# Seven products of halves in the first 16 feature tiles of a down projection

## The chip, the core and the metric

The kernel runs on one core of a Trainium2 chip. The metric is the device time of one execution in microseconds (us), as the median of several runs. TensorE multiplies into PSUM, VectorE and ScalarE read PSUM and work on SBUF, GpSimd (POOL in the profile) works on SBUF, and SyncE (SP) issues DMAs. GpSimd and ScalarE can issue DMAs too.

## What is computed

A trunk of two layers on a sequence of 1024 tokens of width 1024. Each layer is a mixer (two kinds of recurrent heads, which the change does not touch) and a gated MLP with a causal convolution of width 3:

```python
def conv_ffn(h, w_gate, w_val, conv_w, conv_b, w_down):
    a = h @ w_gate
    S = a.shape[1]
    ap = jnp.pad(a, ((0, 0), (CONV_WIDTH - 1, 0), (0, 0)))
    acc = conv_b[None, None, :] + ap[:, 0:S] * conv_w[0]
    for j in range(1, CONV_WIDTH):
        acc = acc + ap[:, j:j + S] * conv_w[j]
    return (jax.nn.silu(acc) * (h @ w_val)) @ w_down
...
    for l in range(DEPTH):
        ...
        h = rms_norm(x, norm2_w[l]) * (1.0 + sc2) + sh2
        x = x + g2 * conv_ffn(h, w_gate[l], w_val[l], conv_w[l], conv_b[l], w_down[l])
    return rms_norm(x, final_norm_w)
```

The hidden width is 2816, or 22 feature tiles of 128. The last product, with `w_down` (2816 by 1024), is the down projection; its result times the gate g2 is added to the residual x.

## The kernel before

Everything is kept feature-major: a tile has 128 features on the partitions and tokens along the row. 512 tokens make a half and fill one PSUM bank. Each float32 operand is split into a high and a low part (fp32r), and each product is three matmuls per 128 rows of contraction: high by high, high by low, low by high.

Two large operand stores hang on this: `hhi`/`hlo` (sliced into b11, b12, b21, b22, each four tiles of 512) and `thi`/`tlo` (`tops[1]` to `tops[3]`, also four tiles of 512 each). Twelve work tiles of 128 by 1024, called z0 to z11, are handed out first in, first out.

The first projection of the MLP takes feature tiles 2 to 21 as pairs: `pair` forms one column block of `w_gate` and one of `w_val` by seven products of halves (`product`, L451 to L453, 12 matmuls each) instead of eight. The sums of weights that this needs are formed on GpSimd (L463 to L469), then `piece` rounds each weight half on ScalarE (L329) and takes the low part on VectorE (L330). There are six buffers for such pieces and two for raw weights. Each product's bank is read by a VectorE add (L485). `conv_act` (L954 to L965) does convolution, silu and the product of the two, and writes the feature tile to DRAM (L966, `acts`).

The down projection then works over the 22 feature tiles in three groups, of 8, 8 and 6. For a group, `take` (L1004) reads its tiles back and `fill_slot` rounds each on ScalarE (L531) and subtracts on VectorE (L532) into places of the operand stores. For each of 8 column blocks d, `stage` loads and splits the weights; `slot_mm` (L526 to L528) runs 24 matmuls into one bank per half; `resid` (L912) multiplies by the gate and adds into `xs[d]`, eight of the z tiles that hold the residual, loaded by GpSimd (L906). Four tiles of group 1 are filled while group 0 runs, the rest after it; group 2 (`dn_last`) likewise.

A scheduler sets the order of instructions on each engine from the order of the code and from priorities; `hp()` marks work that may go ahead. On each engine the instructions then run strictly in that order, so one that waits holds back those behind it. `tick()` feeds in work on the next layer's modulation (L163 to L167).

## Time and profile before

| | us |
|---|---|
| median of 3 runs | 2645.06 (2643.67 to 2646.84) |
| span of the profiled execution | 2637.6 |
| TensorE busy | 2519.4 |
| VectorE busy | 1839.7 |
| ScalarE busy | 986.1 |
| GpSimd busy | 592.0 |

The profile covers one execution; its span runs from the first to the last instruction, and its own time is not listed beside it. The span is 7.5 us below the median of the runs. In names, `f` is the first projection, `dn` groups 0 and 1 of the down projection, `dn_last` group 2, `whi`/`wlo` the high and low weight pieces, `raw` raw weights. A matmul row lasts longer than the step to the next, because matmuls overlap.

### The profile page before, as it was taken

The page shows a single profiled execution, that of the slowest core. Times are in us where ns is not written, and L with a number is a line of the kernel's source. Part 1 is how long each engine was busy: PE and PEld are TensorE (multiplying, and loading weights), DVE is VectorE, ACT ScalarE, POOL GpSimd, SP SyncE. Part 2 cuts the span into 40 slices and gives each one's busy share as a digit, 9 for nine tenths or more (in the row PEclk, how much of TensorE's full clock was granted, in tenths as well). Part 3 has the DMA queues.
Part 4 walks back from the last instruction along what each step waited for, and adds up shares of the span by engine and source line. Part 5 has one row for each costly group of instructions (what it writes and reads, how often), then busy time and mean ns, then how long its engine had stood idle before and what let it go on. Part 6 is the DMA issues. An engine that isn't in the chain of part 4 may idle for free.

```text
span 2637.6 us, 32740 instructions
## 1 busy us (share of the span) xinstructions
PE 2519.4 (96%) x12189; PEld 2072.7 (79%) x12189; DVE 1839.7 (70%) x2781; ACT 986.1 (37%) x1685; POOL 592.0 (22%) x480
## 2 busy tenths in 40 slices
PE   5889999999999999899999899999999999999998
PEld 4777877877788888788877788888877888887887
DVE  6988788765987788834377777777387677674435
ACT  4533433333533333412264334444154333342224
POOL 1512223210423323200023222222033332320000
PEclk8999999999999999999999999999999999999999
DMA  8222322552234344732231112224212222254213
GB/s 293 69 86 86 104 77 82 174 187 80 71 121 132 126 140 151 245 125 94 86 108 56 50 39 64 73 73 160 92 56 76 84 76 88 80 198 138 96 53 107
DMA packets 293920, 283.56 MB, mean 108 GB/s; under 512 B 10793, under 2 KB 240769, under 8 KB 293761
## 3 DMA queue, kind: packets, MB, share of 16 engines
q1 hardware_dynamic: 275904, 219.42, 26.7%
q0 software_dynamic: 17408, 61.88, 6.5%
q8 instruction: 96, 1.57, 0.2%
q14 instruction: 63, 0.52, 0.1%
q10 hardware_dynamic: 449, 0.17, 0.0%
HBM read 229.00 MB, written 52.43 MB: 107 GB/s over the span
## 4 chain that ended last, share of the span: by engine, by line
PE 71%; DVE 12%; issue 10%; POOL 4%; DMA 2%; ACT 2%; POOLq 0%; SPq 0%; DVEq 0%; ACTq 0%
PE f L451 6%; PE f L453 6%; PE f L452 6%; PE dn L528 4%; PE dn L526 4%; PE dn L527 4%; PE lh L712 2%; PE wo L526 2%; PE wo L528 2%; PE wo L527 2%; PE g L451 2%; PE g L452 2%; PE g L453 2%; PE dn_last L526 2%; PE dn_last L528 2%
## 5 line engine op out<-in xcount | busy, mean ns | idle before, releaser
L451 PE MATMUL f<-hhi,whif 128*128 128x512 f32 x640 | 253.8, 397 | 1.9 <-DVE z L485 1.8
L453 PE MATMUL f<-hhi,wlof 128*128 128x512 f32 x640 | 251.4, 393 | 0.0
L452 PE MATMUL f<-hlo,whif 128*128 128x512 f32 x640 | 250.1, 391 | 0.0
L485 DVE TENSOR_TENSOR z<-z,f 128x512 f32<-128x512 f32 x238 | 161.5, 682 | 63.1 <-PE f L453 54.0
L451 PE MATMUL f<-thi,whif 128*128 128x512 f32 x480 | 190.2, 396 | 6.0 <-ACT z L491 4.0
L452 PE MATMUL f<-tlo,whif 128*128 128x512 f32 x480 | 190.0, 396 | 0.0
L453 PE MATMUL f<-thi,wlof 128*128 128x512 f32 x480 | 189.7, 395 | 0.0
L528 PE MATMUL dn<-hhi,wlodn 128*128 128x512 f32 x384 | 151.8, 395 | 9.8 <-DVE wlodn L330 9.8
L526 PE MATMUL dn<-hhi,whidn 128*128 128x512 f32 x384 | 151.6, 395 | 0.0
L527 PE MATMUL dn<-hlo,whidn 128*128 128x512 f32 x384 | 150.1, 391 | 0.0
L167 DVE SCALAR_TENSOR_TENSOR ac<-aw,cact,ac 128x512 f32<-128x512 f32 x140 | 130.7, 934 | 22.8 <-DMA aw<-in_ada_w_dram 22.0
L912 DVE SCALAR_TENSOR_TENSOR z<-dn,mod,z 128x512 f32<-128x512 f32 x64 | 48.0, 750 | 136.3 <-PE dn L528 136.1
L453 PEld LDWEIGHTS f<-hhi,wlof 128*128 128x128 f32 x640 | 120.7, 189 | 28.4
L451 PEld LDWEIGHTS f<-hhi,whif 128*128 128x128 f32 x640 | 120.5, 188 | 28.3 <-DVE z L485 2.3
L452 PEld LDWEIGHTS f<-hlo,whif 128*128 128x128 f32 x640 | 120.6, 188 | 26.9
L451 PEld LDWEIGHTS f<-thi,whif 128*128 128x128 f32 x480 | 90.6, 189 | 29.7 <-ACT z L491 4.9
L915 POOL DMA_DIRECT2D xd<-z x48 | 26.0, 541 | 390.4 <-DVE z L912 362.5
L329 ACT ACTIVATE whidn<-rawdn 128x512 fp32r<-128x512 f32 x64 | 39.5, 627 | 186.1 <-PE dn L527 173.3
L453 PEld LDWEIGHTS f<-thi,wlof 128*128 128x128 f32 x480 | 90.6, 189 | 20.9
L452 PEld LDWEIGHTS f<-tlo,whif 128*128 128x128 f32 x480 | 90.2, 188 | 20.6
L712 PEld LDWEIGHTS lh<-z,z 128*128 128x128 f32 x640 | 80.1, 199 | 24.1 <-issue 19.6
L712 PE MATMUL lh<-z,z 128*128 128x64 f32 x640 | 80.1, 280 | 17.1 <-DVE z L731 16.3
(664 smaller groups left out, 6868.7 us busy)
## 6 DMA issues: line engine op xcount, KB each, us to landing
aw<-in_ada_w_dram SPq DMA_DIRECT2D x160, 256.0 KB, 2.7
acts<-z POOLq DMA_DIRECT2D x44, 512.0 KB, 3.2
z<-acts SPq DMA_DIRECT2D x44, 512.0 KB, 4.3
z<-xd POOLq DMA_DIRECT2D x32, 512.0 KB, 5.7
rawdn<-in_w_down_dram SPq DMA_DIRECT2D x32, 512.0 KB, 3.8
xd<-z POOLq DMA_DIRECT2D x52, 256.0 KB, 2.7
rawdn_last<-in_w_down_dram SPq DMA_DIRECT2D x32, 384.0 KB, 3.4
af<-in_ada_w_dram SPq DMA_DIRECT2D x16, 512.0 KB, 9.9
```

The lines of the kernel that those rows point to most:

```text
L167: V.scalar_tensor_tensor(out=a, in0=raw, scalar=cact[:, k:k + 1], in1=a, op0=ALU.mult, op1=ALU.add)
L329: A.activation(hi[:, 0:n], src, AF.Copy)
L451: T.matmul(ps, wh, rh, start=k == 0, stop=False)
L452: T.matmul(ps, wh, rl, start=False, stop=False)
L453: T.matmul(ps, wl, rh, start=False, stop=k == 3)
L485: V.tensor_add(o, x, ps)
L526: T.matmul(ps, a, rh, start=i == 0, stop=False)
L527: T.matmul(ps, a, rl, start=False, stop=False)
L528: T.matmul(ps, b, rh, start=False, stop=i == last)
L712: T.matmul(ps[:, c * 64:(c + 1) * 64].rearrange("p (b t) -> p b t", t=s), k.t[:, cs], qp.t[:, cs].rearrange("p (b t) -> p b t", t=s)[:, 1: ...
L912: V.scalar_tensor_tensor(out=x, in0=ps, scalar=mod[:, l * 48 + gate + d:][:, 0:1], in1=x, op0=ALU.mult, op1=ALU.add)
L915: nc.gpsimd.dma_start(out=dst[d, :, sl], in_=x)
```

## The change

Groups 0 and 1 of the down projection (16 of the 22 tiles) no longer go by `slot_mm`. Their contraction is cut into even and odd feature tiles, the columns into the two blocks of a pair, the tokens into halves; a pair of column blocks then takes seven products of 12 matmuls. Three PSUM banks are used per pair: x sums products 1, 6, 7 and 4, y sums 5 and 3, z holds 2. After each product VectorE adds the bank as it stands into a part of the residual.

The seven operands made of activations are prepared in `conv_act`, once both tiles of an even and odd pair are there: three differences on VectorE, one on GpSimd, and seven DMAs of 512 columns to a new DRAM tensor `opds`. The six tiles of group 2 still go to `acts`. The seven weight operands come from `pair_weights`, which was cut out of `pair` (its own order of pieces stays) and reads the weights woven, even and odd blocks of 128 columns apart. `fill_operand` loads an operand in two tiles and rounds them into one of the seven operand stores. In the last block of group 0, each store is filled for group 1 after its product.

```diff
-    acts = [dram.tile([FT, P, S], F32, name=f"acts{i}") for i in range(DEPTH)]
+    acts = [dram.tile([GROUPS[-1], P, S], F32, name=f"acts{i}") for i in range(DEPTH)]
+    opds = [dram.tile([P, 7, NOPD, HALF], F32, name=f"opds{i}") for i in range(DEPTH)]
...
+        of = {1: a11, 2: a12, 3: a12, 4: a22, 5: s1, 6: a11, 7: a21}
+        w = {}
         with hp():
-            p1 = piece(a11, HALF, nm + "1")
+            w[1] = piece(a11, HALF, nm + "1")
             G.tensor_add(s1, a21, a22)
             G.tensor_sub(a21, a11, a21)
             G.tensor_sub(a11, s1, a11)
...
+            for i in order[1:]:
+                if i == 3:
+                    G.tensor_sub(a12, a12, a11)
+                w[i] = piece(of[i], HALF, f"{nm}{i}")
+        return w
...
+    def add_product(ps, w, b, first=True):
+        for k in range(4):
+            (wh, wl), rh, rl = w[k], b[0][:, k, :], b[1][:, k, :]
+            T.matmul(ps, wh, rh, start=first and k == 0, stop=False, skip_group_check=True)
+            T.matmul(ps, wh, rl, start=False, stop=False, skip_group_check=True)
+            T.matmul(ps, wl, rh, start=False, stop=k == 3, skip_group_check=True)
...
+            u = kept.pop(i)
+            u0, u1 = u.t[:, 0:HALF], u.t[:, HALF:S]
+            spill(2, lo)
+            spill(3, hi)
+            za, zb = Z(), Z()
+            t5, t6, t7, t4 = za.t[:, 0:HALF], za.t[:, HALF:S], zb.t[:, 0:HALF], zb.t[:, HALF:S]
+            V.tensor_sub(t5, u1, u0)
+            G.tensor_sub(t7, hi, u1)
+            V.tensor_sub(t6, hi, t5)
+            V.tensor_sub(t4, lo, t6)
+            for p, t in ((5, t5), (6, t6), (7, t7), (4, t4)):
+                spill(p, t)
...
+        order7 = (1, 2, 6, 5, 7, 3, 4)
+        t1, t2, t3 = tops[1], tops[2], tops[3]
+        homes = [dict(zip(order7, h)) for h in ((b11, t2, b21, t3, b12, t1, b22), (b11, t2, t3, t1, b21, b12, b22))]
...
+        def fill_operand(gi, p):
+            home = homes[gi][p]
+            for k in (0, 2):
+                raw = Z()
+                dst = [t[:, k:k + 2, :].rearrange("p k n -> p (k n)") for t in home]
+                with hp():
+                    nc.sync.dma_start(out=raw.t[:, :].rearrange("p (k n) -> p k n", k=2),
+                                      in_=opds[l][:, p - 1, gi * 4 + k:gi * 4 + k + 2, :])
+                    fill_slot(dst, raw.t)
+                raw.free()
...
+        fill_operand(0, 1)
+        fill_operand(0, 2)
+        w = down_weights(0, 0)
+        for p in order7[2:]:
+            fill_operand(0, p)
...
+        for gi in range(len(GROUPS) - 1):
+            for j in range(4):
...
+                for i, p in enumerate(order7):
+                    bank = {2: z, 5: y, 3: y}.get(p, x)
+                    add_product(bank, w[p], homes[gi][p], p in (1, 2, 5))
+                    with hp():
+                        resid(bank, *{1: (d1, 0), 2: (d1, 0), 6: (d1, 1), 5: (d2, 1), 7: (d2, 1),
+                                      3: (d1, 1), 4: (d2, 0)}[p], 40)
                     tick()
...
+                    if j == 3:
+                        if gi + 1 < len(GROUPS) - 1:
+                            fill_operand(gi + 1, next(q for q in order7 if homes[gi + 1][q] is homes[gi][p]))
+                        elif i in (1, 2, 3):
+                            fill_last(2 * i - 2)
+                            fill_last(2 * i - 1)
+                    if i == 2:
+                        if j < 3:
+                            more_w = down_weights(gi, j + 1)
```

On VectorE, where layer 0 goes from the pairs into the down projection, before (`f0_21` is the last pair, `hlo`/`tlo` from a z tile a fill, `wlodn` a low piece, L955 and L957 the convolution, L912 a residual add):

```order
L510 TENSOR_TENSOR z3_72<-z3_72,f0_21_5_8457 128x512
L532 TENSOR_TENSOR tlo_502<-z4_73,thi_501 128x1024
L485 TENSOR_TENSOR z3_72<-z3_72,f0_21_3_8478 128x512
L330 TENSOR_TENSOR wlodn0_0_0_4_8515<-rawdn0_0_0_8508,whidn0_0_0_4_8514 128x512
L532 TENSOR_TENSOR hlo_89<-z11_80,hhi_88 128x1024
L955 SCALAR_TENSOR_TENSOR z1_70<-z3_72,cols3_657,z1_70 128x1023
```

The same place in the change (L518 is L510 of before, L547 the fill, L493 the add of the pairs, L927 the residual add, L972 and L974 the convolution, L335 the low piece; z4 and z6 are tiles of feature tile 20):

```order
L518 TENSOR_TENSOR z0_69<-z0_69,f0_21_5_8531 128x512
L547 TENSOR_TENSOR hlo_89<-z4_73,hhi_88 128x1024
L493 TENSOR_TENSOR z0_69<-z0_69,f0_21_3_8552 128x512
L547 TENSOR_TENSOR tlo_504<-z6_75,thi_503 128x1024
L547 TENSOR_TENSOR hlo_89<-z2_71,hhi_88 128x1024
L927 SCALAR_TENSOR_TENSOR z11_80<-dn0_0_0_x_8659,mod_100,z11_80 128x512
L972 SCALAR_TENSOR_TENSOR z3_72<-z0_69,cols3_659,z3_72 128x1023
L547 TENSOR_TENSOR hlo_89<-z5_74,hhi_88 128x1024
L974 SCALAR_TENSOR_TENSOR z3_72<-z0_69,cols3_659,z3_72 128x1022
L335 TENSOR_TENSOR wlodn0_0_02_8601<-rawdn0_0_0g_8588,whidn0_0_02_8600 128x512
```

The second low piece of the first weights stood two instructions behind the fill of the late z tile (`tlo` from z4); it now stands six behind that of z6, which takes its place.

On VectorE, where group 0 of layer 0 ends, before (`dn0_0_7_0` is the last column block's first half):

```order
L912 SCALAR_TENSOR_TENSOR z6_75<-dn0_0_7_0_9017,mod_100,z6_75 128x512
L532 TENSOR_TENSOR hlo_89<-z1_70,hhi_88 128x1024
L532 TENSOR_TENSOR hlo_89<-z3_72,hhi_88 128x1024
L330 TENSOR_TENSOR wlodn0_1_2_0_9212<-rawdn0_1_2_9209,whidn0_1_2_0_9211 128x512
L532 TENSOR_TENSOR hlo_89<-z0_69,hhi_88 128x1024
L912 SCALAR_TENSOR_TENSOR z6_75<-dn0_0_7_1_9018,mod_100,z6_75 128x512
```

The same place in the change (`dn0_0_3` is the last block of group 0, x, y and z its banks):

```order
L547 TENSOR_TENSOR hlo_89<-z1_70,hhi_88 128x1024
L927 SCALAR_TENSOR_TENSOR z4_73<-dn0_0_3_z_9085,mod_100,z4_73 128x512
L547 TENSOR_TENSOR tlo_504<-z5_74,thi_503 128x1024
L547 TENSOR_TENSOR tlo_504<-z2_71,thi_503 128x1024
L927 SCALAR_TENSOR_TENSOR z4_73<-dn0_0_3_x_9083,mod_100,z4_73 128x512
L335 TENSOR_TENSOR wlodn0_1_01_9149<-rawdn0_1_0g_9143,whidn0_1_01_9148 128x512
L547 TENSOR_TENSOR hlo_89<-z0_69,hhi_88 128x1024
L927 SCALAR_TENSOR_TENSOR z3_72<-dn0_0_3_y_9084,mod_100,z3_72 128x512
```

Fills stood among the residual adds at the end of group 0 before, and stand there now; there are more of them, one or two between each two residual adds, over two blocks.

## Rows read from the trace of the kernel before

**Rows 1.** The page, busy time of each engine: us, share of the span, instructions.

```profile
PE 2519.4 (96%) x12189; PEld 2072.7 (79%) x12189; DVE 1839.7 (70%) x2781; ACT 986.1 (37%) x1685; POOL 592.0 (22%) x480
```

**Rows 2.** Windows: us; busy of PE, PEld, DVE, ACT, POOL (count); clock; DMA share; GB/s.

```profile
858.00:898.00 40.00, 40.00 (x179) 32.78 (x178) 31.37 (x43) 12.06 (x18) 11.77 (x10) 1.00 0.46 144
...
2180.00:2220.00 40.00, 40.00 (x175) 32.58 (x174) 28.14 (x36) 14.20 (x21) 11.95 (x10) 1.00 0.25 79
...
2460.00:2551.00 91.00, 91.00 (x399) 74.64 (x398) 33.75 (x43) 19.05 (x26) 0.00 (x0) 1.00 0.24 76
...
1098.00:1110.00 12.00, 4.41 (x20) 3.26 (x18) 7.32 (x10) 3.22 (x5) 2.62 (x5) 0.85 0.79 311
```

**Rows 3.** Timeline of TensorE, layer 1: start us, us, engine, line, out<-in, count.

```profile
2180.17 0.39 PE L452 MATMUL f<-tlo,whif 128*128 128x512 f32 x1
...
2344.90 0.39 PE L451 MATMUL f<-hhi,whif 128*128 128x512 f32 x1
...
2380.97 0.39 PE L527 MATMUL dn<-hlo,whidn 128*128 128x512 f32 x1
...
2551.12 0.39 PE L528 MATMUL dn<-hhi,wlodn 128*128 128x512 f32 x1
```

**Rows 4.** The same, both entries and last matmuls; in brackets idle before, releaser.

```profile
1099.01 0.39 PE L526 MATMUL dn<-hhi,whidn 128*128 128x512 f32 x1
...
1110.05 0.79 PE L528 MATMUL dn<-hhi,wlodn 128*128 128x512 f32 x1 [7.64 <-DVE wlodn L330]
1110.64 0.63 PE L526 MATMUL dn<-hhi,whidn 128*128 128x512 f32 x1
...
1285.91 0.39 PE L528 MATMUL dn<-hhi,wlodn 128*128 128x512 f32 x1
...
2370.55 0.39 PE L526 MATMUL dn<-hhi,whidn 128*128 128x512 f32 x1
...
2376.06 0.65 PE L528 MATMUL dn<-hhi,wlodn 128*128 128x512 f32 x1 [2.12 <-DVE wlodn L330]
```

**Rows 5.** The chain that ended last, layer 0's entry: start us, us, what.

```profile
1093.92 6.05 DMA acts<-z
1100.03 6.43 DMA z<-acts
1106.48 1.07 ACT thi L531
...
1109.39 0.61 DVE wlodn L330
```

**Rows 6.** Timeline of VectorE: the late subtraction at both entries.

```profile
1107.57 1.23 DVE L532 TENSOR_TENSOR tlo<-z,thi 128x1024 fp32r<-128x1024 f32 x1 [4.68 <-ACT thi L531]
...
2373.58 1.23 DVE L532 TENSOR_TENSOR tlo<-z,thi 128x1024 fp32r<-128x1024 f32 x1 [3.88 <-ACT thi L531]
```

**Rows 7.** Groups of instructions: busy us, mean ns, idle before (last two: minimum/median/maximum ns).

```profile
L912 DVE SCALAR_TENSOR_TENSOR z<-dn,mod,z 128x512 f32<-128x512 f32 x64 | 48.0, 750 | 136.3 <-PE dn L528 136.1
...
L330 DVE TENSOR_TENSOR wlodn<-rawdn,whidn 128x512 fp32r<-128x512 f32 x64 | 43.7, 686 | 42.7 <-ACT whidn L329 42.7
...
L329 ACT ACTIVATE whidn<-rawdn 128x512 fp32r<-128x512 f32 x64 | 39.5, 627 | 186.1 <-PE dn L527 173.3 <-DMA rawdn<-in_w_down_dram 12.0 <-PE f L452 0.9
...
L955 DVE SCALAR_TENSOR_TENSOR z<-z,cols,z 128x1023 f32<-128x1023 f32 x44 | 58.5, 1330 | 22.3 <-ACT z L954 22.1
...
L532 DVE TENSOR_TENSOR hlo<-z,hhi x9: 1217/1220/1226, 1100.5 to 1199.3; 128x1024 fp32r<-128x1024 f32 x9
L531 ACT ACTIVATE hhi<-z x8: 1041/1064/1067, 1107.4 to 1197.3; 128x1024 fp32r<-128x1024 f32 x8
```

**Rows 8.** Timeline of VectorE and of GpSimd, a low piece beside a weight sum.

```profile
2346.97 1.47 DVE L330 TENSOR_TENSOR wlof<-rawf_21v,whif 128x512 fp32r<-128x512 f32 x1
...
2346.60 1.29 POOL L469 TENSOR_TENSOR rawf_21g<-rawf_21g 128x512 f32<-128x512 f32 x1 [2.14 <-DVE wlof L330]
```

**Rows 9.** The page, DMA issues: count, size, median us from issue to landing.

```profile
rawdn<-in_w_down_dram SPq DMA_DIRECT2D x32, 512.0 KB, 3.8
```

More of the change, by code (lines that the diff above doesn't have):

```diff
@@ L31 @@
 GROUPS = (8, 8, 6)
+NOPD = sum(GROUPS[:-1]) // 2
 WAIT_F, WAIT_POOL, WAIT_ROT, WAIT_ST, WAIT_OUT = 7, 1, 1, 2, 3
@@ L454, in product, with pair_weights @@
         return ps
-    def pair(src_g, src_v, nm, plain_first=False):
+    def pair_weights(src_g, src_v, nm, order, woven=False):
         rg = load_raw(src_g, KT, nm + "g")
@@ L465, in pair @@
             G.tensor_sub(a11, s1, a11)
-            if not plain_first:
-                p6 = piece(a11, HALF, nm + "6")
-            p2 = piece(a12, HALF, nm + "2")
-            G.tensor_sub(a12, a12, a11)
-            if plain_first:
-                p3 = piece(a12, HALF, nm + "3")
-                p6 = piece(a11, HALF, nm + "6")
-            p7 = piece(a21, HALF, nm + "7")
-            p4 = piece(a22, HALF, nm + "4")
-            p5 = piece(s1, HALF, nm + "5")
-            if not plain_first:
-                p3 = piece(a12, HALF, nm + "3")
+            for i in order[1:]:
[3 more added lines that the diff above has]
+        return w
+    def pair(src_g, src_v, nm, plain_first=False):
+        w = pair_weights(src_g, src_v, nm, (1, 2, 3, 6, 7, 4, 5) if plain_first else (1, 6, 2, 7, 4, 5, 3))
+        p1, p2, p3, p4, p5, p6, p7 = (w[i] for i in range(1, 8))
         need(2)
@@ L965, in conv_act @@
                     V.tensor_mul(tmp.t, v.t, tmp.t)
-            nc.gpsimd.dma_start(out=acts[l][ft], in_=tmp.t)
-            tmp.free()
+            if ft >= 2 * NOPD:
+                nc.gpsimd.dma_start(out=acts[l][ft - 2 * NOPD], in_=tmp.t)
+                tmp.free()
+                return
+            i = ft // 2
+            lo, hi = tmp.t[:, 0:HALF], tmp.t[:, HALF:S]
+            spill = lambda p, src: nc.gpsimd.dma_start(out=opds[l][:, p - 1, i, :], in_=src)
+            if ft % 2 == 0:
+                kept[i] = tmp
+                spill(1, lo)
+                return
+            u = kept.pop(i)
[10 more added lines that the diff above has]
+                spill(p, t)
+            for t in (u, tmp, za, zb):
+                t.free()
         parts = [(w_gate, l, 0, f"f{l}_0g"), (w_val, l, 0, f"f{l}_0v")]
@@ L1002, in take, with fill_last @@
+        starts = [sum(GROUPS[:i]) for i in range(len(GROUPS))]
+        last_ops = []
+        def fill_last(i):
             raw = Z()
             with hp():
-                nc.sync.dma_start(out=raw.t, in_=acts[l][f])
-                fill_slot(dst, raw.t)
+                nc.sync.dma_start(out=raw.t, in_=acts[l][i])
+                fill_slot(last_places[i], raw.t)
             raw.free()
-            return dst
-        fresh = (GROUPS[0], 4, 2)
-        starts = [sum(GROUPS[:i]) for i in range(len(GROUPS))]
@@ L1011 @@
-        groups = [[] for _ in GROUPS]
-        def fill(gi, a, b):
-            for i in range(a, b):
-                groups[gi].append(take(starts[gi] + i, places[gi][i]))
-        xs = []
-        for gi, n in enumerate(GROUPS[:-1]):
-            dw = lambda d: stage(w_src(w_down, l, d * P, starts[gi], n), n, f"dn{l}_{gi}_{d}")
-            if gi == 0:
-                fill(0, 0, 2)
-                w = dw(0)
-                fill(0, 2, n)
-                load_xs(0, xd[2 * l + 1])
-            else:
-                w = dw(0)
-            fill(gi + 1, 0, fresh[gi + 1])
-            for d in range(KT):
-                if gi == 0 and d + 1 < KT:
-                    load_xs(d + 1, xd[2 * l + 1])
-                pss = [pr_ps(f"dn{l}_{gi}_{d}_{half}") for half in range(2)]
-                for half in range(2):
-                    slot_mm(pss[half], w, groups[gi], half)
-                    tick()
-                w = dw(d + 1) if d + 1 < KT else None
-                for half in range(2):
-                    resid(pss[half], d, half, 40)
-            fill(gi + 1, fresh[gi + 1], GROUPS[gi + 1])
+            last_ops.append(last_places[i])
@@ L1072 @@
                 ps = pr_ps(f"{nm}_{d}_{half}")
-                slot_mm(ps, w, groups[-1], half)
+                slot_mm(ps, w, last_ops, half)
                 resid(ps, d, half, 40, xd[2 * l + 2] if more else None)
```

33 lines of the change are left out of this document (28 added, 5 removed).

## The prediction

> **What bounds the kernel now.** I read the page first, then the busy time of single stretches, then TensorE's rows at both ends of the down projection, then the chain that ended the only pause there. TensorE is busy 96% of the span [rows 1]. Four stretches show what that share is made of [rows 2]: in the pairs of the first projection (layer 0 at 858, layer 1 at 2180) and in the down projection itself (2460 to 2551) TensorE is busy all the time at the full granted clock, while VectorE has 31.4, 28.1 and 33.8 us of work in 40, 40 and 91 us. The fourth stretch, 1098 to 1110, is the entry into the down projection of layer 0: TensorE works 4.4 of 12 us, the clock is 0.85, and the DMA share is 0.79.
>
> The pace of one matmul comes from start times, since the ends are modelled. In the down projection of layer 1, 739 steps lie between 2380.97 and 2551.12: 0.2302 us each. In the pairs, 713 steps lie between 2180.17 and 2344.90: 0.2310 us each [rows 3]. None of these steps is a pause, although the pairs already change their product, their PSUM bank and their weights every 12 matmuls.
>
> The 768 matmuls of groups 0 and 1 start at 1099.01 in layer 0 and the last one at 1285.91; in layer 1 it is 2370.55 and 2551.12 [rows 4]. At pace, 767 steps take 176.6 us; the stage took 186.9 and 180.6. So the entry loses 10.3 us in layer 0 and 4.0 us in layer 1. The rows show how: 14 matmuls, then a wait for a low weight piece (7.64 and 2.12 us), then some nine matmuls at half clock (0.6 us long where 0.39 is usual), which cost about 1.7 us. Behind the wait in layer 0 is a chain [rows 5]: the feature tile of 20 is written out (6.05 us), read back (6.43), rounded on ScalarE (1.07), subtracted on VectorE [rows 6], and the piece stands behind that on VectorE. In layer 1 the same subtraction starts at 2373.58 after 3.88 us of idling.
>
> **The change, part by part.** *Fewer matmuls.* A pair of column blocks and halves takes seven products of 12 instead of eight: 672 for 768 per layer, 192 rows fewer on TensorE in the program. The new stage repeats the pattern of the pairs, so I give it their pace: 672 x 0.2310 = 155.2 us against 768 x 0.2302 = 176.8, a gain of 21.6 per layer, 43.2 in all. This lies on the path, as TensorE does not pause there.
>
> The Trainium skill (TensorE: Matmul & The Clock Gate, Back-to-back issue gap) gives about 131 ns as the sustained step at 512 columns. By that the 192 matmuls would be worth only 25 us (an estimate from that page); the rows here step by 0.23, so the sum goes by 0.2302.
>
> *Residual adds and weight pieces.* Each product is added into the residual, 7 adds per block of two column blocks where 4 stood: 112 for 64, at 0.75 us. Pieces rise from 64 to 112 too, at 0.69 us on VectorE and 0.62 on ScalarE [rows 7]. Per block of 84 matmuls (19.4 us) VectorE has 7 x 0.75 + 7 x 0.69 = 10.1 us and ScalarE 4.3. Both hide under TensorE, and I cost them at nothing. Without that cover the 48 more of each would be 69 us. Bank x takes four products, y two; the next product in a bank must wait until VectorE has read the one before. One product in another bank (2.77 us) lies between, and the read takes 0.75: hidden unless the read is over 2.0 us late.
>
> *GpSimd.* Four sums per block now run beside this, 64 in all, at about 1.3 us. What they do to VectorE is in the trace: a low piece that overlaps one takes 1.47 us instead of 0.69 [rows 8]. Four such cost 3.1 us per block: 13.2 of 19.4, still hidden.
>
> *Operands in the first projection.* For 16 feature tiles per layer, a pair of tiles adds three subtractions on VectorE (2.1 us per 39 us), one on GpSimd and five DMA issues on its queue. In layer 0 VectorE has 8.6 us idle in 40 [rows 2]. I put 1 us in all on this, bounds 0 and 4; all of it exposed would be 16 x 2.1 = 33 us.
>
> *Entry.* Fourteen fills are needed instead of eight, but in the order of the seven products; only the first operand is due at once. That part helps: product 1 can follow the last pair directly. The piece of product 2, however, now stands further back on VectorE, behind the late subtraction and six more instructions (the order on VectorE in the section on the change). By hand, layer 0: the late subtraction ends at 1107.57 + 1.22 = 1108.8. The next fill needs ScalarE, which starts at 1106.48 and has three roundings of 1.06 and a piece of 0.62 before it: 1110.3. Then fill 1.22, residual 0.75, convolution 1.33, fill 1.22, convolution 1.33, piece 0.69 [rows 7]: 1116.9. TensorE can run 12 + 6 matmuls from 1099.0, to 1103.2. A pause of 13.7, and 1.7 for the clock after it: 15.4, against 10.3 now. The same chain from 2373.58 ends at 2382.9 in layer 1; TensorE is there at 2374.7. A pause of 8.2, and 1.7: 9.9, against 4.0. So the entries cost 5.1 + 5.9 = 11 us more. Bounds: 0, if the new order of need repays the later piece; 17, if each entry meets one more queued transfer of 3 us.
>
> *Group turns.* Group 1's seven operands are filled between the products of the last block of group 0 and the first block of group 1: 14 fills of 1.22 over 38.8 us, with four free tiles to load into, as eight hold the residual. VectorE then has 17.1 + 20.2 = 37.3 of 38.8 us: nearly full. On VectorE one fill stands ahead of the residual of the first product, which makes it some 2.3 us late (1.06 + 1.22), 0.3 more than its slack. In the kernel before, fills also stand ahead of residual adds at this turn without a pause on TensorE. I take 2 us per turn, 4 in all; bounds 0 and 10 (next part).
>
> *Sum.* -43.2 + 11 + 4 + 1 = -27. The profiled execution has a span of 2637.6 us, 7.5 less than the median of 2645.06; I take what lies around the span as unchanged. Span 2610.4, time **2618**.
>
> **Rivals.** (1) *The entry costs no more than now.* Product 1 covers 2.8 us and the operands come one by one. For it: a shorter first need. Against it: the queue on VectorE. -43.2 + 5 = 2607; with the turns free as well 2602.
>
> (2) *VectorE becomes the bound at the turns and the entries.* With GpSimd's overlap the turn has 18.6 + 3.1 = 21.7 us of VectorE work in a block of 19.4: 2.3 x 4 blocks = 9.3, and the entries, where fills, pieces and residuals meet too, another 5 each: -43.2 + 11 + 1 + 9.3 + 10 = -12, 2633. For it: the low piece of 1.47 us [rows 8]. Against it: it needs nearly every GpSimd sum to hit VectorE.
> The Trainium skill (SBUF — State Buffer, Who interferes with whom) says that a VectorE instruction with two SBUF inputs and a reading GpSimd instruction exclude each other, and the loser waits for the whole instruction. By that rule this would be the likely case, with up to 4 x 1.3 us per block; the trace agrees in kind, with 0.8 us [rows 8].
>
> (3) *Slower: the weights come too late in every block.* Raw weights have two buffers, so the second half of the next weights can load only 4.1 us into a block; then the load (median 3.8 [rows 9]), three GpSimd sums (1.3 each), ScalarE and VectorE: its piece is ready at 13.1, and the residual of the fifth product stands behind it on VectorE. TensorE needs that bank at 16.6. So each block waits for what a load takes beyond some 6.5 us. With 14 blocks after a first, 1.9 us more each eats the 27; at 11 us per load it is 4.5 x 14 = 63, time 2681. Against it: the pairs load as much at the same rate, with 713 steps and no pause [rows 3], and the read-back at the crowded entry took 6.43 [rows 5].
>
> That the change does not do what it says is excluded: the program has 9804 rows on TensorE for 9996.
>
> **How the numbers follow.** Forecast (2611 to 2626) 0.56; rival 1 0.17; rival 2 0.19; rival 3 0.06; 0.02 for anything else. A measurement of this kernel tells about 0.2% (5.3 us) from no change. The forecast, rival 1 and most of rival 2 are faster by more: 0.87; the rest of rival 2 within: 0.06; slower: 0.07. The range takes in rival 1 with free turns (2602) and rival 2 with its bounds: 2600 to 2642.
>
> **What would show it.** The stage between the first and last matmul of groups 0 and 1 should take about 172 us in layer 0 and 167 in layer 1. Right: one pause of some 13 us in layer 0 and 8 in layer 1, after the first 18 matmuls, ended by a low piece of VectorE; steps of 0.231 elsewhere; small pauses ended by residual adds around the turn. Wrong: pauses in every block ended by a residual add or a piece (rival 3), a row of pauses over two blocks at the turns (rival 2), no pause after the 18 (rival 1), or new pauses in the pairs before.

## The result: 0.5% slower

| | before | after |
|---|---|---|
| median, us (4 runs each) | 2644.36 (2640.69 to 2646.84) | 2657.43 (2654.14 to 2661.99) |
| span of the profiled execution | 2637.6 | 2654.4 |
| layer 0: pairs of the first projection | 404.4 | 427.4 |
| layer 0: groups 0 and 1 of the down projection | 187.1 | 183.8 |
| layer 1: pairs | 392.5 | 396.2 |
| layer 1: groups 0 and 1 | 180.8 | 176.3 |

The ratio is 1.0052, with a 95% interval of 1.0039 to 1.0064. In every run whose span is listed the time is 1.7 to 2.2 us above the span, which puts the profiled execution of before at some 2639.4 us (an estimate), 5 us below its median: by medians the change costs 13.1 us, by the two spans 16.8. A stage is counted from its first matmul to the first matmul of the next stage; the stages not listed differ by 3 us or less each and by -2 together.

The page of the kernel after, the busy line (it answers [rows 1]) and two groups of matmuls; the last two figures are the idle time before them and what ended it:

```profile
PE 2497.5 (94%) x11997; PEld 2041.6 (77%) x11997; DVE 2023.9 (76%) x2949; ACT 1036.3 (39%) x1757; POOL 752.8 (28%) x640
...
L456 PE MATMUL f<-hhi,whif 128*128 128x512 f32 x640 | 255.1, 399 | 13.4 <-DVE z L493 11.1
...
L526 PE MATMUL dn_x<-hhi,whidn 128*128 128x512 f32 x224 | 90.2, 402 | 11.1 <-DVE z L927 9.1
```

The 192 matmuls are gone (12189 to 11997), but TensorE's share fell from 96 to 94%: it waits for VectorE, for the adds of the products in the pairs (L493) and about as much for the residual adds in the down projection (L927). VectorE has 184 us more.

Windows of the kernel after (columns as in [rows 2]): the pairs of layer 0 at the stretch of [rows 2], those of layer 1, and the group turn of layer 1:

```profile
851.00:891.00 40.00, 38.34 (x169) 30.75 (x169) 35.58 (x44) 12.77 (x20) 16.17 (x16) 1.00 0.47 150
891.00:931.00 40.00, 37.43 (x160) 30.19 (x159) 33.71 (x43) 13.01 (x20) 15.61 (x16) 0.96 0.44 140
...
2198.00:2238.00 40.00, 40.00 (x175) 32.58 (x174) 32.29 (x40) 14.18 (x21) 15.26 (x16) 1.00 0.30 99
2478.00:2518.00 40.00, 35.04 (x147) 26.91 (x146) 33.98 (x35) 16.16 (x22) 12.32 (x8) 1.00 0.58 195
```

Before, the pairs of both layers had TensorE at 40.00. Now only layer 1's have, with VectorE at 32.29 for 28.14. Layer 0 has VectorE at 34 to 36, and in the second stretch, with a pause of 2.57 us at 908.55, the granted clock reads 0.96. TensorE's rows after, in order: two pauses of layer 0's pairs, layer 0's entry, layer 1's entry, its turn, and 261 rows from 2508.93 to the last:

```profile
824.51 0.57 PE L456 MATMUL f<-thi,whif 128*128 128x512 f32 x1 [2.00 <-DVE z L493]
...
908.55 0.47 PE L456 MATMUL f<-hhi,whif 128*128 128x512 f32 x1 [2.57 <-DVE z L493]
...
1127.55 0.80 PE L526 MATMUL dn_y<-thi,whidn 128*128 128x512 f32 x1 [5.19 <-ACT thi L546]
...
1132.29 0.79 PE L526 MATMUL dn_x<-hhi,whidn 128*128 128x512 f32 x1 [2.43 <-DVE z L927]
...
1136.42 0.80 PE L528 MATMUL dn_z<-thi,wlodn 128*128 128x512 f32 x1 [2.90 <-DVE wlodn L335]
...
2400.44 0.80 PE L527 MATMUL dn_y<-tlo,whidn 128*128 128x512 f32 x1 [3.37 <-DVE tlo L547]
...
2405.23 0.79 PE L528 MATMUL dn_z<-thi,wlodn 128*128 128x512 f32 x1 [2.90 <-DVE wlodn L335]
...
2504.38 0.50 PE L526 MATMUL dn_y<-hhi,whidn 128*128 128x512 f32 x1 [1.60 <-DVE z L927]
...
2508.93 0.39 PE L528 MATMUL dn_x<-hhi,wlodn 128*128 128x512 f32 x1
...
2568.83 0.39 PE L528 MATMUL dn_x<-hhi,wlodn 128*128 128x512 f32 x1
```

The last two give the pace of the new stage: 59.90 us for 260 steps, 0.2304. In the pairs of layer 0, with the modulation of layer 1 still running there, there are some fifteen such pauses, of 0.4 to 2.6 us; in the kernel before there is none after the first pairs.

### The profile page after: what moved, and what is told of

It is laid out like the page before. It is cut to its first block, busy times and chain, and to the rows that moved or that the text cites. A ratio compares the mean times of both kernels' runs of the same rounds, so it can differ in the third digit from the quotient of the medians.

```text
span 2654.4 us, 33080 instructions
## 1 busy us (share of the span) xinstructions
PE 2497.5 (94%) x11997; PEld 2041.6 (77%) x11997; DVE 2023.9 (76%) x2949; ACT 1036.3 (39%) x1757; POOL 752.8 (28%) x640
## 4 chain that ended last, share of the span: by engine, by line
PE 63%; DVE 16%; issue 11%; POOL 4%; DMA 3%; ACT 3%; POOLq 0%; DVEq 0%; SPq 0%; ACTq 0%
PE f L456 5%; PE f L458 5%; PE f L457 5%; PE lh L727 2%; PE wo L541 2%; PE wo L543 2%; PE wo L542 2%; PE g L456 2%; PE g L458 2%; PE g L457 2%; PE dn_last L541 2%; PE dn_last L543 2%; PE dn_last L542 2%; PE dn_x L526 2%; PE dn_x L528 2%
## 5 line engine op out<-in xcount | busy, mean ns | idle before, releaser
L493 DVE TENSOR_TENSOR z<-z,f 128x512 f32<-128x512 f32 x238 | 161.3, 679 | 18.2 <-PE f L458 15.1
L456 PEld LDWEIGHTS f<-hhi,whif 128*128 128x128 f32 x640 | 120.7, 189 | 44.3 <-ACT whif L334 10.8
L168 DVE SCALAR_TENSOR_TENSOR ac<-aw,cact,ac 128x512 f32<-128x512 f32 x140 | 137.4, 982 | 19.9 <-DMA aw<-in_ada_w_dram 18.9
L971 ACT ACTIVATE z<-z,cols,cols 128x1024 f32<-128x1024 f32 x44 | 54.6, 1242 | 121.1 <-DVE z L493 111.4
L526 PE MATMUL dn_x<-hhi,whidn 128*128 128x512 f32 x224 | 90.2, 402 | 11.1 <-DVE z L927 9.1
L727 PEld LDWEIGHTS lh<-z,z 128*128 128x128 f32 x640 | 80.8, 200 | 23.8 <-issue 19.2
L727 PE MATMUL lh<-z,z 128*128 128x64 f32 x640 | 80.8, 281 | 16.8 <-DVE z L746 15.7
L527 PE MATMUL dn_x<-hlo,whidn 128*128 128x512 f32 x224 | 88.3, 394 | 1.7 <-DVE hlo L547 1.7
L528 PE MATMUL dn_x<-hhi,wlodn 128*128 128x512 f32 x224 | 88.1, 393 | 0.0
L927 DVE SCALAR_TENSOR_TENSOR z<-dn_x,mod,z 128x512 f32<-128x512 f32 x64 | 47.8, 746 | 39.6 <-PE dn_x L528 39.2
```

Source lines behind the costliest of these rows:

```text
L168: V.scalar_tensor_tensor(out=a, in0=raw, scalar=cact[:, k:k + 1], in1=a, op0=ALU.mult, op1=ALU.add)
L456: T.matmul(ps, wh, rh, start=k == 0, stop=False)
L493: V.tensor_add(o, x, ps)
L526: T.matmul(ps, wh, rh, start=first and k == 0, stop=False, skip_group_check=True)
L527: T.matmul(ps, wh, rl, start=False, stop=False, skip_group_check=True)
L528: T.matmul(ps, wl, rh, start=False, stop=k == 3, skip_group_check=True)
```

## Experiments on layer 0's pairs

The question is why these pairs got 23.0 us longer where the prediction had 1. My first theory was that VectorE has too much work there; its rivals were the write-outs on GpSimd's queue and the DMA traffic. Single runs are given with the run of the kernel before on the same chip in brackets. On one chip single runs of the kernel before lay between 2631.1 and 2644.5, so the readings go by stages and rows more than by such totals.

**Parts of the new work.** Three subtractions of VectorE left out, their plain halves written out instead; and the other way round, the four subtractions alone in the kernel before, their results unused:

```diff
-            V.tensor_sub(t5, u1, u0)
             G.tensor_sub(t7, hi, u1)
-            V.tensor_sub(t6, hi, t5)
-            V.tensor_sub(t4, lo, t6)
-            for p, t in ((5, t5), (6, t6), (7, t7), (4, t4)):
+            for p, t in ((5, u1), (6, hi), (7, t7), (4, lo)):
```

> The changed kernel without the three subtractions of halves on VectorE (the plain halves are written out in their place, so three of the seven operands hold other values; every transfer, the GpSimd subtraction and the whole down projection stay). Theory: in layer 0 the in-order VectorE, which also makes layer 1's modulation there, is over-full with the three subtractions, each drawn out by GpSimd's sums from 0.68 to 1.3-1.9 us; without them layer 0's pairs go back from 427 to 404-409 us and the whole run is 2633-2640 us. Rival A, the seven write-outs per two tiles on GpSimd's queue, which stand between the sums of the weights and make the weight pieces late: the pairs stay at 420 us or more and the run at 2650-2658. Rival B, the DMA traffic itself: as rival A.

> The kernel before with only the four subtractions of halves added (three on VectorE, one on GpSimd, their results thrown away; the write-outs stay the old ones, the down projection is the old one). Theory: layer 0's pairs grow by 12-23 us from 404, layer 1's by 0-2, the run is 2657-2668. Rival A (the write-outs on GpSimd's queue): under 4 us more in all, 2643-2648.

Without VectorE's subtractions: 2642.19 (2637.13), pairs 419.5. With the four subtractions alone, added to the kernel before: 2656.40 (2637.13), pairs 421.4. So the subtractions suffice for 17 of the 23 us, as expected, but what is left without VectorE's three (one GpSimd subtraction and five more write-outs per two tiles) costs 15 by itself, which was not. Either addition uses up something that both need. In the kernel without the subtractions it isn't VectorE's throughput: between 740 and 1000 us VectorE is busy 207 us there, against 213 in the kernel before, which has no pause in that time. In the kernel after it is busy 228 of the 260 us, some 18.6 per pair where the matmuls take 19.4 (an estimate from these windows and the periods below), so there its load alone leaves little. VectorE's in-order waits for rounded weight pieces, 720 to 1040 us (total, times, longest), are longer without the subtractions than before, and shorter in the kernel after, which has less idle time. The kernel before, the one after, and the one without the subtractions:

```profile
DVE wlof L330 <- ACT whif L329: 44.8, 16, 4.2
```

```profile
DVE wlof L335 <- ACT whif L334: 27.8, 10, 4.3
```

```profile
DVE wlof L335 <- ACT whif L334: 52.1, 15, 5.0
```

**GpSimd's queue.** The write-outs moved to SyncE's queue; or kept on GpSimd and, with GpSimd's subtraction, held back behind its weight sums, so that none stands between them:

```diff
-            spill = lambda p, src: nc.gpsimd.dma_start(out=opds[l][:, p - 1, i, :], in_=src)
+            spill = lambda p, src: nc.sync.dma_start(out=opds[l][:, p - 1, i, :], in_=src)
```

```diff
+    def flush():
+        s = last_sum[0]
+        with tc.issue_after(s.ins if hasattr(s, "ins") else s):
+            for fn in due:
+                fn()
+        due[:] = late
+        late.clear()
...
-                spill(1, lo)
+                late.append(lambda: spill(1, lo))
```

> The changed kernel with the seven write-outs of each two tiles issued from SyncE's queue instead of GpSimd's. Theory (VectorE over-full by the subtractions): layer 0's pairs stay at 420 us or more, the run at 2650-2660, or later still, as SyncE's in-order queue now holds loads behind a write-out that waits for its tile. Rival A (GpSimd's queue makes the weight sums late): the pairs come back to 404-412 us, the run to 2634-2643.

> The changed kernel with the write-outs and the GpSimd difference of each two tiles held back on GpSimd's queue, each time until the three sums of the next weights but one have been issued; the same work, in another place of one queue. New theory (two causes that add on one chain: the sums of the next weights come later because of the write-outs between them, and VectorE, which waits in order for the low part of piece 6, holds the pairs' residual adds): layer 0's pairs come down from 427 to 411-419 us, the run to 2641-2649. The old theory alone (only VectorE's load): 423 us or more, 2653 or more.

2657.53 (2637.13), pairs 434.7; and 2664.24 (2634.29), pairs 434.0. Both are longer than the changed kernel's 427.4. Each move can cost something of its own, so the totals alone don't decide it. But held back, the write-outs do let the loop described below go faster (10.1 us from the seventh low part to piece 6, for 10.8), and the pairs got longer all the same: the write-outs between the sums are not the cause, and my second theory fell here.

**The modulation of layer 1**, which in layer 0 runs on VectorE beside the pairs: its second half moved to layer 1; made at half the rate up to tile 15 and kept away from the entry and the turn of the down projection (the first of the places is shown); left out, with its loads and small matmuls.

```diff
-            ada_todo.extend((l + 1, b) for b in range(12))
+            ada_todo.extend((l + 1, b) for b in range(6))
...
+            ada_todo.extend((l, b) for b in range(6, 12))
```

```diff
     def step():
-        tick()
+        beat[0] += 1
+        if not (thin[0] and beat[0] % 2):
+            tick()
```

```diff
-            ada_todo.extend((l + 1, b) for b in range(12))
+            V.memset(mod[:, 48:96], 0.25)
+            V.memset(modA[:, 16:32], 1.25)
```

> The changed kernel with the second six of the twelve column blocks of layer 1's modulation moved out of layer 0's pairs into the start of layer 1. Theory: the pauses of layer 0's pairs stay up to about the tenth pair, while the modulation's first half is still made, and are gone from there on: 8-12 us fewer in the pairs, 0-4 us more in layer 1, 2646-2653 in all. Rival A (GpSimd's queue) and rival B (DMA traffic): pauses go on in the pairs of 890-1010 us as before, 2654-2659 in all.

> The changed kernel with layer 1's modulation made at half the rate in layer 0's pairs up to tile 15, at the full rate after, and in the down projection away from its entry and its turn; what is left goes to layer 1's first stage. VectorE's load as a cause: layer 0's pairs 405-413 us, its down projection 178-182 us (from 183.8), layer 1's first stage up to 5 us longer, 2636-2646 in all. The write-outs as the only cause: 420 us or more, 2650 or more.

> The changed kernel without layer 1's modulation (constants in its place; its loads, its 96 multiply-adds on VectorE and its 48 small matmuls are left out). Layer 0 is then as layer 1 is in the changed kernel. If VectorE's load is one of two causes that must meet: layer 0's pairs 393-399 us (layer 1's are 396), its down projection 176-179, 2616-2624 in all. If the write-outs delay the sums enough by themselves: 405 us or more in the pairs.

Half moved: 2644.17 (2637.13), pairs 414.5, down projection 178.3. Half rate: 2651.62 (2634.29), pairs 413.1, but its down projection took 189.2 for the 178 to 182 expected, and the whole is above the 2636 to 2646. Left out: 2623.03 (2634.29), pairs 396.2, as in layer 1. With half of it moved, the last multiply-add of the modulation in these pairs (VectorE's timeline) and TensorE's windows around it show that the pauses end soon after it (the pairs' last is one of 0.58 us at 968.90):

```profile
943.94 3.15 DVE L168 SCALAR_TENSOR_TENSOR ac<-aw,cact,ac 128x512 f32<-128x512 f32 x2
```

```profile
891.00:931.00 40.00, 36.65 (x161) 29.03 (x160) 34.11 (x42) 13.19 (x20) 16.53 (x16) 1.00 0.44 144
931.00:971.00 40.00, 37.84 (x163) 30.14 (x162) 34.67 (x43) 13.08 (x20) 16.07 (x16) 1.00 0.43 141
971.00:1011.00 40.00, 40.00 (x174) 32.55 (x174) 32.23 (x40) 13.31 (x20) 15.69 (x16) 1.00 0.31 100
```

And a window of the kernel without it, with all the new work in place:

```profile
851.00:891.00 40.00, 40.00 (x175) 32.57 (x174) 31.62 (x38) 14.95 (x23) 15.79 (x16) 1.00 0.31 100
```

So the new work and the modulation must meet. The stretched subtractions alone are not enough: without the modulation they take as long, 1.4 to 1.7 us each on average, and cause no pause. **How little room there was** can be read in the kernel before. The seventh weight piece of a pair, that of product 3, takes over the buffer of its first, and only when VectorE has made its low part can the next raw gate weights load. Pair 8 (that of feature tile 8), kernel before: its second product starts at 821.94, and the low part (`rawf_8g`) at 825.65, 3.7 us behind (TensorE's and VectorE's timelines):

```profile
821.94 0.40 PE L451 MATMUL f<-thi,whif 128*128 128x512 f32 x1
```

```profile
823.06 0.68 DVE L330 TENSOR_TENSOR wlof<-s1f,whif 128x512 fp32r<-128x512 f32 x1
824.45 1.29 DVE L955 SCALAR_TENSOR_TENSOR z<-z,cols,z 128x1023 f32<-128x1023 f32 x1 [0.71 <-ACT z L954]
825.65 0.69 DVE L330 TENSOR_TENSOR wlof<-rawf_8g,whif 128x512 fp32r<-128x512 f32 x1
```

The same pair after: the second product starts at 824.51 (the first pause shown above), the low part at 832.27, 7.8 us behind; modulation, adds of products and a convolution stand ahead of it:

```profile
824.28 1.16 DVE L335 TENSOR_TENSOR wlof<-rawf_8v,whif 128x512 fp32r<-128x512 f32 x1
825.37 0.74 DVE L168 SCALAR_TENSOR_TENSOR ac<-aw,cact,ac 128x512 f32<-128x512 f32 x1
826.61 0.75 DVE L168 SCALAR_TENSOR_TENSOR ac<-aw,cact,ac 128x512 f32<-128x512 f32 x1 [0.50 <-DMA aw<-in_ada_w_dram]
827.27 0.68 DVE L493 TENSOR_TENSOR z<-z,f 128x512 f32<-128x512 f32 x1
...
829.67 0.69 DVE L335 TENSOR_TENSOR wlof<-s1f,whif 128x512 fp32r<-128x512 f32 x1
831.07 1.28 DVE L972 SCALAR_TENSOR_TENSOR z<-z,cols,z 128x1023 f32<-128x1023 f32 x1 [0.71 <-ACT z L971]
832.27 0.68 DVE L335 TENSOR_TENSOR wlof<-rawf_8g,whif 128x512 fp32r<-128x512 f32 x1
```

The same two rows of pairs 5 to 14, as means, us; the period is the mean step from a pair's first matmul to the next pair's:

| kernel, layer | pairs | period | lag of the seventh low part |
|---|---|---|---|
| before, 0 | 404.4 | 19.9 | 4.0 (5.4 in pair 3, 1.8 in pair 5, then unevenly up to 6.7 in pairs 17 and 19) |
| before, 1 | 392.5 | 19.4 | 0.7 |
| after, 0 | 427.4 | 21.3 | 6.2 |
| after, 1 | 396.2 | 19.4 | 1.0 |
| before and the subtractions, 0 | 421.4 | 20.7 | 6.2 |
| after without VectorE's subtractions, 0 | 419.5 | 21.0 | 5.7 |
| after without the modulation, 0 | 396.2 | 19.4 | 1.2 |

In the kernel before, VectorE fell behind in the course of layer 0 and TensorE didn't feel it. From the low part on, loading, GpSimd's sums and the next pair's piece of product 6 take 10.0 to 11.0 us in every kernel of this table; VectorE waits in order for that piece with the pair's adds behind it. The first of these sums starts 4.5 us after the low part before, and 4.8 after (4.7 in layer 1): neither the DMA traffic nor the modulation's loads make the raw weights late, so that rival falls as well.

**Attempts to shorten that loop.** The last two products of a pair exchanged with their pieces (the pieces are shown), so that the raw buffer comes free a product earlier; and the value weights, whose buffer is free earlier, loaded first; each also in the kernel before.

```diff
-        w = pair_weights(src_g, src_v, nm, (1, 2, 3, 6, 7, 4, 5) if plain_first else (1, 6, 2, 7, 4, 5, 3))
+        w = pair_weights(src_g, src_v, nm, (1, 2, 3, 6, 7, 4, 5) if plain_first else (1, 6, 2, 7, 4, 3, 5))
```

```diff
-        rg = load_raw(src_g, KT, nm + "g")
+        if woven:
+            rg = load_raw(src_g, KT, nm + "g")
         rv = load_raw(src_v, KT, nm + "v")
+        if not woven:
+            rg = load_raw(src_g, KT, nm + "g")
```

> The changed kernel with the pairs' third product made, and its weight piece cut, before the fifth (the last two change places), so that the buffer of raw weights comes free one product, 2.8 us, earlier. Theory of the loop (raw buffer free, load of 4.5 us, GpSimd's sums, piece 6, VectorE waiting for it in order with the residual adds behind; its slack in layer 0 is used up by the subtractions and the modulation): 2.8 us more slack per pair take most pauses away, layer 0's pairs 404-412 us, 2634-2643 in all. Theory of VectorE's throughput alone (too much work per pair): 420 us or more, 2650 or more.

> The kernel before with the same swap of the third and fifth product. Its pairs run at the pace of the matmuls already (404 and 393 us): no change is expected by either theory, 2634-2646, unless the order of the last two pieces costs something by itself.

> The changed kernel with one pair of lines changed: in the pairs the value weights, whose buffer comes free about two products before the other's, are loaded first, so that only the gate weights' load follows the last piece. Theory of the loop (seventh piece's low part on VectorE, raw buffer free, two loads one after the other, GpSimd's sums, piece 6's low part, VectorE's queue up to the next seventh piece; in layer 0 it takes 21.6 us a pair against 19.7 for the matmuls): it loses about 2 us, comes to 19.5, and layer 0's pairs to 404-409 us; layer 1's stay at 396; 2633-2642 in all. Theory of VectorE's throughput, or of the write-outs: 420 us or more, 2650 or more.

> The kernel before with the same two lines changed. Its pairs already run at the pace of the matmuls; by the loop theory only its reserve grows: the low part of the seventh piece, now 4.0 us behind the first product on average and falling further behind from pair to pair, stays 1-3 us behind; no change in all, 2634-2644.

Exchange: 2699.35 after and 2672.74 before (2636.63), pairs 436.4 and 411.6; the mixers, which use the same pairs, also got longer by 11 to 17 us each. Why the exchange costs so much was not followed up. Value weights first: 2652.73 (3 runs), ratio to before 1.0055 (1.0012 to 1.0098), pairs 425.2, lag 6.3; in the kernel before 2640.04, ratio 1.0020 (1.0008 to 1.0031), lag 3.2, pairs 407.8. The first three miss; the last stays in its range of time, at a lag just over the 1 to 3 us. In the changed kernel the value weights first brought only layer 1's pairs back, to 392.9; in layer 0 the loop was hardly shorter (10.6 us for 10.8, period 20.9). VectorE's instructions were drawn out in another place: in that kernel, one subtraction (first fence, VectorE) starts with a GpSimd sum and ends after two (second fence, GpSimd); the eight of its line in layer 0 average 3.2 us:

```profile
969.61 3.11 DVE L1006 TENSOR_TENSOR z<-z,z 128x512 f32<-128x512 f32 x1
```

```profile
969.60 1.31 POOL L479 TENSOR_TENSOR rawf_15g<-s1f,rawf_15g 128x512 f32<-128x512 f32 x1
970.85 1.31 POOL L1004 TENSOR_TENSOR z<-z,z 128x512 f32<-128x512 f32 x1
```

In the changed kernel the three subtractions average (groups of VectorE, 691 to 1119 us; busy us, mean ns):

```profile
L1000 DVE TENSOR_TENSOR z<-z 128x512 f32<-128x512 f32 x8 | 10.6, 1320 | 0.0
L1003 DVE TENSOR_TENSOR z<-z,z 128x512 f32<-128x512 f32 x8 | 10.2, 1271 | 0.0
L1002 DVE TENSOR_TENSOR z<-z,z 128x512 f32<-128x512 f32 x8 | 9.9, 1232 | 0.0
```

That is 1.2 to 1.3 us where the prediction put 0.7.

**The modulation moved for good**: four blocks from tile 14 on, where no differences are made any more, eight into layer 1's mixer; and the same move in the kernel before.

```diff
-            ada_todo.extend((l + 1, b) for b in range(12))
+            pass
...
-            if l == 0 and h == 0:
-                ada_todo.extend((0, b) for b in range(4, 12))
+            if h == 0:
+                ada_todo.extend((l, b) for b in range(4, 12))
...
+            if l + 1 < DEPTH and ft == 14:
+                ada_todo.extend((l + 1, b) for b in range(4))
```

> The changed kernel with layer 1's modulation moved out of layer 0's pairs that make differences: its first four blocks from the 14th tile on, the other eight in layer 1's first stage, as layer 0 has its own. If the modulation on VectorE, together with the new work, is what makes the loop longer than the matmuls: layer 0's pairs 398-405 us (from 427), its down projection 176-179, layer 1's first stage 5-12 us longer; 2630-2640 in all. If something else holds the pairs: 415 us or more, 2650 or more.

> The kernel before with the modulation moved in the same way: what the move is worth without the change. Its pairs are at the matmuls' pace already and lose the modulation's own interruptions: 397-401 us for 404; layer 1's first stage 5-12 us longer; 2636-2648 in all, no measurable change. So e13_ada_moved against this one is the change's own worth where VectorE has room: 5-12 us faster.

After: 2635.29, ratio to before 0.9989 (0.9975 to 1.0002), pairs 400.2 as expected, at a period of 19.4 and a lag that stays at 4.2. Before with the move: 2635.75, ratio 0.9991 (0.9977 to 1.0004), pairs 397.2. The waits of TensorE, 720 to 1060 us, of the changed kernel and of the changed kernel with the move:

```profile
PE f L456 <- DVE z L493: 12.3, 9, 2.6
PE f L456 <- DVE z L518: 1.9, 2, 1.1
```

```profile
PE f L456 <- DVE z L493: 2.4, 2, 1.6
```

Apart from the modulation the new work in the pairs costs 3 us a layer, 6 in all, where the prediction had at most 4; it falls on a stage's first pairs, as the period from pair 5 on is 19.4 in both kernels. But the change gains nothing even then, where I expected 5 to 12 us. Its down projection of layer 0 took 183.6, for the 176 to 179 expected, and the modulation's last multiply-adds still fell into it (1115 to 1147 us, its entry's pauses up to 1128). That of layer 1, with no modulation, took 177.3. So with the pairs mended, the entries and turns alone still use up all but 3 us of what the fewer matmuls gain (360.9 us in both layers, for 364.0 in the kernel before with the move).

## Experiments on the down projection

GpSimd's sums left out; or made on VectorE, in all blocks:

```diff
+            if woven:
+                of[5] = a12
+            else:
+                G.tensor_add(s1, a21, a22)
...
```

```diff
-            G.tensor_add(s1, a21, a22)
+            E = V if woven else G
+            E.tensor_add(s1, a21, a22)
...
```

> The changed kernel without GpSimd's four weight sums per block in the down projection (the unsummed halves are cut in pieces in their place). If VectorE's instructions, drawn out beside GpSimd's sums, bind the entries and the turn (the second rival of the prediction): layer 1's down projection goes from 176.3 to 167-171 us, and the turn's 5 us of pauses to 1-2. If the chain of loads and splits of operands binds them: 174-177 us.

> The changed kernel with the down projection's weight sums on VectorE instead of GpSimd. VectorE then has 32 x 4 sums more per layer pair of groups, 0.68 us each where nothing stands beside them, but none of its instructions is drawn out there. If the drawing-out costs more than the sums themselves: each layer's down projection 2-6 us shorter (178-182 and 171-174 us), 2648-2654 in all. If the entries and the turn are bound by VectorE's own load: 0-6 us longer, 2656-2668 in all.

Left out: 2631.65 (2634.29); 175.8 us in layer 0 and 169.2 in layer 1, 8.0 and 7.1 less, 169.2 as expected for VectorE's drawn-out instructions. Layer 1's turn: two low weight pieces on VectorE and the sums on GpSimd in the kernel after, then the same two pieces without the sums, and the window of that turn:

```profile
2500.18 3.49 DVE L335 TENSOR_TENSOR wlodn<-rawdn_1g,whidn 128x512 fp32r<-128x512 f32 x2
```

```profile
2499.69 1.73 POOL L474 TENSOR_TENSOR s1dn<-rawdn_1v 128x512 f32<-128x512 f32 x1 [15.31 <-DMA rawdn_1v<-in_w_down_dram]
2501.50 1.62 POOL L475 TENSOR_TENSOR rawdn_1v<-rawdn_1g,rawdn_1v 128x512 f32<-128x512 f32 x1
```

```profile
2477.90 1.29 DVE L335 TENSOR_TENSOR wlodn<-rawdn_1g,whidn 128x512 fp32r<-128x512 f32 x2
```

```profile
2461.00:2501.00 40.00, 40.00 (x176) 32.58 (x175) 29.94 (x40) 17.14 (x23) 0.00 (x0) 1.00 0.54 182
```

Beside two sums the two pieces take 3.49 us instead of 1.29, and the turn's pauses (6.2 us in layer 1 by TensorE's rows from 2483 to 2509) are gone without them. The entries are not: TensorE without the sums, layer 0's entry and layer 1's:

```profile
1123.71 0.79 PE L529 MATMUL dn_y<-thi,whidn 128*128 128x512 f32 x1 [6.82 <-ACT thi L549]
1128.56 0.79 PE L529 MATMUL dn_x<-hhi,whidn 128*128 128x512 f32 x1 [2.80 <-DVE z L930]
1132.68 0.80 PE L531 MATMUL dn_z<-thi,wlodn 128*128 128x512 f32 x1 [2.90 <-DVE wlodn L335]
...
2384.48 0.80 PE L530 MATMUL dn_y<-tlo,whidn 128*128 128x512 f32 x1 [3.35 <-DVE tlo L550]
2389.26 0.79 PE L531 MATMUL dn_z<-thi,wlodn 128*128 128x512 f32 x1 [2.90 <-DVE wlodn L335]
```

They are the pauses of the kernel after, at the same places and hardly shorter. Of the 15.1 us gained, some 12 to 13 come from the turns and 2 to 3 from the entries. Leaving the sums out also takes them out of the chain from load to piece; with the sums on VectorE they stay in it, and there the turns shrink as well, which points to GpSimd's overlap. In all, though, the sums on VectorE (64, not the 32 x 4 of the expectation) were no gain: 2655.41 (2636.63), 185.2 and 179.3, with one pause of 18.6 and 15.5 us at the entries, ended by a low piece, where VectorE now had the first blocks' sums ahead of their pieces; the turns shrank to 1.8 and 1.9 us. Three kernels put edits together; the second and third keep the first two blocks' sums on GpSimd:

```diff
+            E = V if woven and nm[-3:] not in ("0_0", "0_1") else G
```

> Three changes at once to the changed kernel: the swap of the third and fifth product in the pairs, the down projection's weight sums on VectorE, and six of the twelve blocks of layer 1's modulation made in layer 1's first stage. If the loop and the drawing-out are the causes: layer 0's pairs 400-406 us, its down projection 172-176, layer 1's 171-174, first stage of layer 1 0-5 us longer: 2616-2632. If VectorE's throughput is the cause: 2635-2645.

> The changed kernel with the value weights loaded first, the down projection's weight sums on VectorE except in its first two blocks, and the last two of the twelve blocks of layer 1's modulation made in layer 1's first stage, so that none is left for the entry of layer 0's down projection. Layer 0's pairs 403-408, its down projection 172-178, layer 1's 171-175, layer 1's first stage 0-3 us longer: 2618-2632. If the drawn-out instructions cost no more than the sums on VectorE: the down projections stay at 176-184 and the whole at 2632-2640.

> As e13_ada_moved, and with the value weights of the pairs loaded first and the down projection's weight sums on VectorE except in its first two blocks. Layer 0's pairs 398-404, the down projections 171-175 each; 2618-2632 in all, 6-12 us under e13_ada_moved.

The first (exchange, all sums on VectorE, half of the modulation moved): 2677.12 (2636.63); its down projections took 174.1 and 174.4, about as expected, its pairs 421.1, as the exchange costs more than the rest brings. The second (value weights first, two blocks of modulation moved): 2644.40, ratio 1.0025 (1.0007 to 1.0044), down projections 178.2 and 171.9, pairs 422.5: the down projections close to what was expected, the pairs not. The third, with the modulation moved as above: **2631.41**, ratio to before 0.9976 (0.9966 to 0.9987); pairs 401.1, down projections 177.7 and 172.6. It is 7.0 us (0.2%) under the kernel before on its chip (2638.45), and by the ratios under the kernel after too, but only 3.9 under the kernel with the move alone, where 6 to 12 were expected.

## Why the prediction was wrong

By span, the forecast was -27 and the result +16.8 (-27 and +13.1 by medians; what lies around the span is 1.8 us, and not the 7.5 that the prediction took as unchanged). Its terms (they sum to +19.2; the stages the change does not touch took 2 us less):

- **Fewer matmuls, -43.2: right.** 192 rows fewer, pace 0.2304. The 131 ns of the Trainium skill (TensorE: Matmul & The Clock Gate, Back-to-back issue gap) don't show here either.
- **Operands in the first projection, +1 (bounds 0 and 4): +26.6, the step that failed.** 23.0 in layer 0, 3.6 in layer 1. I read "VectorE has 8.6 us idle in 40" as room. The idle time was mostly in-order waiting inside a loop (44.8 of 58 us idle, in 16 waits for rounded pieces, above), and the lag of up to 6.7 us stood in the trace of before. The price of a subtraction was off too: 1.2 to 1.3 us, not 0.7. "All of it exposed would be 33" was the better bound. I had said new pauses in the pairs would prove me wrong; they did.
- **Entries, +11 (15.4 and 9.9): 22.4 and 15.4, against 10.3 and 4.0 before, so +23.5.** The first part came as worked out: the pauses and slow matmuls up to the piece of product 2 sum to some 16 in layer 0 and 10 in layer 1. Left out was what follows: VectorE comes out of the entry late, and the next residual adds and fills hold TensorE another 5 to 6 us in each layer. The pause was not one after 18 matmuls but several (three over 2 us in layer 0, two in layer 1), since TensorE met late operands first, in layer 0 after 14 matmuls; that their sum agrees is in part luck. With the turns this term missed by 21 us, nearly as much as the pairs. No run here tests an edit meant for the entries' own chain of loads and fills, so what would shorten them stays open.
- **Group turns, +4: +12.3**, 6.1 and 6.2 each. The 3.1 us per block for GpSimd's overlap that the second rival added was the right correction here: without the sums the turns' pauses are gone.
- **The second rival** gave +15 over the forecast, 5 for the turns and 10 for the entries. Leaving the sums out gained 15.1, but that the two agree is luck: nearly all of it came from the turns. There its mechanism holds and deserved more than 0.19; for the entries it does not. The Trainium skill (SBUF — State Buffer, Who interferes with whom) says that VectorE's second pair of ports is shared with GpSimd under an exclusive lock; the trace agrees: 2.2 us more on two pieces, 2.4 on one subtraction.
- **The third rival**, weights too late in each block, did not occur in the down projection: away from entry and turn it steps at pace.

What is shown: without the modulation beside it the new work costs layer 0's pairs 3 us, with it 23, and each half of the new work alone 15 to 17. That this goes through VectorE's in-order loop is argued from the rows. What stays open is the single step of the loop that binds: three edits meant to shorten it failed, and more buffers for raw weights or pieces, meant to cut it, were not tried.

## What to carry to other kernels

Idle time on an in-order engine is room only if nothing waits behind its waits. Before adding work there, follow one recurring instruction from iteration to iteration: if its lag behind TensorE grows, as from 1.8 us in pair 5 to 6.7 in pair 17 here, there is little room, whatever the busy share; a lag that stayed, the 4.2 us with the modulation moved, went with no pause. Price a VectorE instruction on two SBUF operands by its row beside GpSimd's work, and look at each layer: the one with other work on that engine paid 23 us, the other 3.6.

## What the hardware showed

VectorE can lose to two GpSimd instructions in a row: 3.11 us for a subtraction that takes 0.68 where nothing overlaps it. GpSimd's sums stretch as well, 1.6 to 1.7 us at the turn for 1.3. And in the kernel after, the granted clock of the stretch from 891 to 931 reads 0.96 (its levels are 1.2 and 2.4 GHz). TensorE's only pause over 0.4 us there is that of 2.57 us before 908.55; from 910.4 to 913.4 its matmuls then step by 0.43 us instead of 0.23. In the stretch before, with two pauses of 0.81 and 0.84 us, it reads 1.00.
